# Scratch of the sample values laid out by batch: four loads a head in place of eight

## The chip, the cores and the metric

The kernel runs on one core of a Trainium2 chip. The metric is device time in microseconds for one whole execution. Engines are named as the profile names them: PE (TensorE, matrix products), DVE (VectorE), ACT (ScalarE), POOL (GpSimd) and SP (SyncE). In this kernel SP does no arithmetic: it issues the DMA transfers, one after the other, in the order in which they stand in its program.

## What is computed

One layer of a decoder step with two branches. A shared projection of the normed input gives, per head, queries, keys and values; the second branch keeps a matrix memory per head and advances it. Cut to what matters here:

```python
proj = jnp.einsum('btd,dn->btn', hn, w_in)
a_pool, z_pool, q, k, v, o, z_m, i_pre, f_pre, g_pool, g_mlstm = split_projection(proj)
...
kw = k * w_state[..., None]
C_new = decay[..., None, None] * C + jnp.einsum('bhsd,bhsv->bhdv', kw, v)
n_new = decay[..., None] * n + jnp.sum(kw, axis=2)
```

There are 528 prompt rows (512 and 16 meta tokens) of one sequence, and a sample group of 8 batches with 4 tokens each. Width 1024, four heads of 512. For the sample group each batch and head has its own state `C` of 512 x 512, read from memory, updated with four tokens and written back.

## The kernel before

Products are made with values split in two parts, a rounded one (`hi`) and the rest (`lo`), and three products hi x lo, lo x hi, hi x hi. So the update of one batch's `C` by its 4 tokens is one matmul over 12 rows: on one side `kwst` (weighted keys), on the other `vst` (values; parts hi, lo, hi, four tokens each):

```python
nc.tensor.matmul(pu, self.kwst[h, d][r:r + 12, g], self.vst[h][r:r + 12, g], start=True, stop=True,
                 tile_position=(r, 0))
```

Here `r` is 32 times the batch number modulo 4, and `g` is 0 for batches 0 to 3 and 1 for batches 4 to 7. So `vst` has four blocks of twelve partitions, and two batches in each.

The work goes head by head. `unit_v(h)` projects a head's values: it loads four pieces of weights (`wraw`), splits them, multiplies, and takes each result out of the accumulator into tiles `v` (`take`). When the last piece is done, five steps follow (`units[3].after`): two calls of `sample_rows`, two of `store` (values to the DRAM tensor `v_d`) and `stack`. The 32 sample rows (8 batches x 4 tokens) stand in two of the `v` tiles: 24 rows for batches 2 to 7 and 8 rows for batches 0 and 1. `sample_rows` splits them (L141 is the DVE half of the split) into tiles `vsp`, and writes hi, lo and hi again to a DRAM scratch `vs_d` of the head (L1013): six stores a head. `stack` reads the scratch into `vst` (L1019): eight loads a head, one for each batch.

Behind the values of a head come the projections of its queries, keys, gates. They are made in units that share one form (`quad`, L187 to 288): the weights come in two halves of 512 KB each, `ra` and `rb` (L196, two transfers). ACT and DVE split and combine them: ACT's casts at L203 and L210 (the first four blocks of `ra`, tile `w`), DVE's differences at L206 and L213 and sums at L216. PE multiplies (L167) in a fixed sequence of products; after some of them ACT copies the accumulator out (L239, tiles `p`, `u`, `e`), and DVE adds two of them up (L252 to 256, tiles `q`, `k`). Beside these units run the updates of the sample state: `C` is loaded (L1117) and stored (`out_dram`, L1149) in pieces of 512 KB, small rows of weights `sw` are loaded (L1040, L1041), and queries and their products go to DRAM (`q_d` L1049, `qc_d` L1167).

PE's order is written out by hand. For the other engines, and so for SP, a scheduler decides the order, from what waits for what and from the estimated lengths of instructions. Each engine then works strictly in its order. A DMA transfer is counted by one of eight semaphores that are taken in turn: a transfer that takes a semaphore waits until the transfer that had it before, eight transfers earlier, has landed.

Of the kernel before, what the change touches and what calls it, by code (L numbers as in the profile page):

```python
# [8 lines left out]
F32 = mybir.dt.float32  # L9
# [15 lines left out]
HD = 512  # L25
NB = 8
# [74 lines left out]
class Trunk:  # L101
# [857 lines left out]
    def unit_v(self, h):  # L959
        nc = self.nc  # L960
        V, A, G = nc.vector, nc.scalar, nc.gpsimd
        pv, vt, w = [], {}, {}

        def load(kk):
            w[kk] = [self.raw("wraw", 2, HD)]
            nc.sync.dma_start(w[kk][0], self.w_in[:, 2 * kk:2 * kk + 2, CV + h * HD:CV + (h + 1) * HD])

        def part(kk, low):
            if not low:
                w[kk] += [self.hl("w" + s, 2, HD) for s in ("hi", "lo")]  # L970
                A.copy(w[kk][1], w[kk][0])
            else:
                V.tensor_tensor(w[kk][2], w[kk][0], w[kk][1].bitcast(F32), ALU.subtract)

        def product(k, i):
            kk, k2 = divmod(k, 2)
            _, wh, wl = w[kk]
            if k == 0:
                pv.append(self.ps())
            if i < 4:  # L980
                c0 = COLS[i][0][2]
                hh, hl = (t[:, k, c0:c0 + P] for t in self.hT)
                for j, (s, m) in enumerate(((hl, wh), (hh, wl), (hh, wh))):
                    nc.tensor.matmul(pv[i], s, m[:, k2], start=(k == 0 and j == 0), stop=(k == 7 and j == 2))  # L984
            else:
                for j, m in enumerate((wl, wh)):
                    nc.tensor.matmul(pv[4][:112], self.hS[:, k], m[:, k2], start=(k == 0 and j == 0),  # L987
                                     stop=(k == 7 and j == 1))
            if k == 7:
                take(i)  # L990

        def take(i):
            t = vt[i] = self.r("v32")
            if i == 4:
                A.copy(t[:48, :HD], pv[4][64:112])
                V.tensor_tensor(t[:48, :HD], pv[4][:48], t[:48, :HD], ALU.add)
                A.activation(t[:48, :HD], t[:48, :HD], AF.Copy, accum_out=t[:48, HD:HD + 1])
            else:
                A.activation(t[:, :HD], pv[i], AF.Copy, accum_out=t[:, HD:HD + 1])

        def store(*rows):
            for i, r0, r1, n0 in rows:
                nc.sync.dma_start(self.v_d[h, n0:n0 + r1 - r0], vt[i][r0:r1, :HD + 1])


        def sample_rows(src, r0, r1, s0, n):
            d = vt.get("d")
            if d is None:
                d = vt["d"] = self.dram.tile([3, 32, HD], F32, name=f"vs_d{h}")
            hi, lo = (self.r("vsp", F32R)[:, :HD] for _ in range(2))  # L1010
            self.split(hi[r0:r1], lo[r0:r1], vt[src][r0:r1, :HD], A, V)
            for j, x in enumerate((hi, lo, hi)):
                nc.sync.dma_start(d[j, s0:s0 + n], x[r1 - n:r1].bitcast(F32))  # L1013

        def stack():
            vst = self.vst[h] = self.wp.tile([P, 2, HD], F32R, tag="vst", name=f"vst{h}", bufs=1)
            for b in range(NB):
                r = 32 * (b % 4)
                nc.sync.dma_start(vst[r:r + 12, b // 4].bitcast(F32), vt["d"][:, 4 * b:4 * b + 4])  # L1019

        units = []
        for kk in range(4):

            products = [lambda k=k, i=i: product(k, i) for k in (2 * kk, 2 * kk + 1) for i in range(5)] if kk < 3 else \
                [lambda k=k, i=i: product(k, i) for i in (4, 3, 0, 1, 2) for k in (6, 7)]
            units.append(Unit([lambda kk=kk: load(kk)], [lambda kk=kk: part(kk, False), lambda kk=kk: part(kk, True)],
                              products))
        units[3].after = [lambda: sample_rows(4, 0, 48, 8, 24), lambda: sample_rows(3, 96, 128, 0, 8),
                          lambda: store((4, 0, 24, 264), (4, 24, 48, 536), (3, 120, 128, 528), (3, 0, 120, 408)),
                          lambda: store((0, 0, 128, 8), (1, 0, 128, 136), (2, 0, 8, 0), (2, 8, 128, 288)), stack]  # L1030
        return units
# [624 lines left out]
```

## Time and profile before

| what | before |
|---|---|
| median of 3 runs | 1132.77 us (1131.75 to 1134.3) |
| profiled execution | 1128.94 us |
| its span, first to last instruction | 1127.2 us |
| mean granted clock of PE | 0.978 |
| PE busy | 1062.4 us, 94% of the span |
| DVE, ACT, POOL busy | 826.4, 542.7, 155.1 us |
| chain of work that ended last | PE 76%, DMA 12%, DVE 4%, ACT 3%, issue 2% |
| projections of the heads | about 60 to 745 us of the span |

The span is what the trace shows; the profiled execution's time includes what lies around it. "Busy" is time in which an engine has an instruction under way. A wait is named by what ended it: "PE ps L167 <- ACT u L239" is PE standing before the product at L167 until ACT's instruction on tile `u` at L239 was done. SP's lines are DMA issues; their length is SP's own time for the issue, and the transfer goes on behind it. The granted clock is the share of full speed that the throttle gave PE.

### The profile page before, as it was taken

How to read it: one execution, taken by the hardware profiler on the slowest of the kernel's cores; microseconds unless marked ns; L12 is line 12 of the kernel's file. 1: busy time of each engine (PE TensorE's matmuls, PEld its weight loads, DVE VectorE, ACT ScalarE, POOL GpSimd, SP SyncE). 2: the span in 40 equal slices, each digit the busy share in tenths (PEclk: the TensorE clock that was granted, in tenths of full speed). 3: DMA queues.
4: the chain of work that ended last, by engine and by line, in shares of the span. 5: the costliest groups of instructions: out<-in, count | busy, mean ns of one | idle time of the engine just before them, and what ended most of it. 6: DMA issues, size and time to landing. Idle time of an engine off the chain costs nothing.

```text
span 1127.2 us, 19656 instructions
## 1 busy us (share of the span) xinstructions
PE 1062.4 (94%) x7390; PEld 957.6 (85%) x7390; DVE 826.4 (73%) x1342; ACT 542.7 (48%) x1027; POOL 155.1 (14%) x309
## 2 busy tenths in 40 slices
PE   6799999999899999999999999987997889999997
PEld 5789999859899869999869989975986789999876
DVE  5778888786689687789696888864788988544343
ACT  5656555334454444454444554455676655122232
POOL 2100120001100001200000300012464423200000
PEclk9899999999999999999999999998999999999999
DMA  9263456789557688557587578888777889423232
GB/s 216 71 184 111 152 157 229 248 281 265 193 172 248 196 297 226 181 179 251 183 265 253 186 225 270 278 269 289 230 236 257 260 296 358 149 76 102 64 94 84
DMA packets 159663, 233.33 MB, mean 207 GB/s; under 512 B 17369, under 2 KB 82133, under 8 KB 159561
## 3 DMA queue, kind: packets, MB, share of 16 engines
q1 hardware_dynamic: 159569, 232.09, 64.1%
q8 instruction: 58, 0.95, 0.4%
q14 instruction: 36, 0.29, 0.1%
HBM read 160.65 MB, written 70.93 MB: 205 GB/s over the span
## 4 chain that ended last, share of the span: by engine, by line
PE 76%; DMA 12%; DVE 4%; ACT 3%; issue 2%; SPq 1%; POOL 1%; POOLq 0%; DVEq 0%; ACTq 0%
PE ps L167 57%; PE ps L984 7%; PE ps L1131 3%; PE ps L1372 2%; DMA wraw<-in_w_in_dram 2%; PE ps L1140 2%; DMA v_d<-v 1%; DMA rb<-in_w_in_dram 1%; DMA ra<-in_w_in_dram 1%; PE ps L987 1%; DMA v<-v_d 1%; DMA k<-k_d 1%; PE ps L1415 1%; PE ps L80 1%; ACT qc L1166 1%
## 5 line engine op out<-in xcount | busy, mean ns | idle before, releaser
L167 PE MATMUL ps<-hT_hi,w 128*128 128x272 f32 (+1 forms) x752 | 159.8, 294 | 0.0
L167 PEld LDWEIGHTS ps<-hT_hi,w 128*128 128x128 f32 x752 | 124.6, 190 | 4.9 <-issue 3.1
L167 PE MATMUL ps<-hT_lo,w 128*128 128x272 f32 (+1 forms) x376 | 109.2, 291 | 0.0
L1145 DVE SCALAR_TENSOR_TENSOR C<-C,sw,ps 128x512 f32<-128x512 f32 x128 | 89.5, 742 | 10.6 <-PE ps L1140 10.2
L167 PE MATMUL ps<-Sc_hi,wa 128*128 128x272 f32 (+1 forms) x376 | 81.0, 295 | 8.0 <-ACT u L239 7.9
L206 DVE TENSOR_TENSOR wb<-rb,wb 128x1024 fp32r<-128x1024 f32 x47 | 57.5, 1223 | 39.3 <-ACT wb L203 39.0
L167 PE MATMUL ps<-hT_hi,wb 128*128 128x272 f32 (+1 forms) x376 | 79.7, 291 | 3.5 <-DVE q L254 3.5
L167 PE MATMUL ps<-Sb_hi,wb 128*128 128x272 f32 (+1 forms) x376 | 80.1, 293 | 2.5 <-ACT p L239 1.9
L203 ACT CAST wa<-ra 128x1024 fp32r<-128x1024 f32 x47 | 49.3, 1049 | 63.8 <-DVE ra L216 56.6
L167 PE MATMUL ps<-Sd_hi,w 128*128 128x272 f32 (+1 forms) x376 | 79.6, 291 | 0.0
L167 PE MATMUL ps<-Sa_hi,wa 128*128 128x272 f32 (+1 forms) x376 | 78.7, 289 | 0.0
L167 PEld LDWEIGHTS ps<-hT_lo,w 128*128 128x128 f32 x376 | 71.3, 190 | 0.0
L167 PEld LDWEIGHTS ps<-Sc_hi,wa 128*128 128x128 f32 x376 | 63.4, 192 | 8.7 <-ACT u L239 8.6
L1054 POOL COPY qm<-qw 128x16 f32<-128x16 f32 x32 | 7.6, 271 | 426.4 <-DVE qw L1051 426.4
L167 PEld LDWEIGHTS ps<-hT_hi,wb 128*128 128x128 f32 x376 | 62.3, 189 | 4.2 <-DVE q L254 4.2
L203 ACT CAST w<-rb 128x1024 fp32r<-128x1024 f32 x47 | 49.3, 1050 | 33.3 <-PE ps L167 17.9
L167 PEld LDWEIGHTS ps<-Sb_hi,wb 128*128 128x128 f32 x376 | 62.3, 189 | 3.3 <-ACT p L239 2.3
L167 PEld LDWEIGHTS ps<-Sd_hi,w 128*128 128x128 f32 x376 | 62.8, 191 | 0.0
L167 PEld LDWEIGHTS ps<-Sa_hi,wa 128*128 128x128 f32 x376 | 62.0, 188 | 0.0
L206 DVE TENSOR_TENSOR w<-rb,w 128x1024 fp32r<-128x1024 f32 x47 | 57.4, 1222 | 3.7 <-ACT w L203 3.6
L206 DVE TENSOR_TENSOR wa<-ra,wa 128x1024 fp32r<-128x1024 f32 x47 | 57.3, 1218 | 0.0
L203 ACT CAST wb<-rb 128x1024 fp32r<-128x1024 f32 x47 | 49.1, 1046 | 15.6 <-DVE rb L216 15.4
(371 smaller groups left out, 3078.3 us busy)
## 6 DMA issues: line engine op xcount, KB each, us to landing
C<-in_state_C_dram SPq DMA_DIRECT2D x64, 512.0 KB
out_dram<-C SPq DMA_DIRECT2D x64, 512.0 KB
ra<-in_w_in_dram SPq DMA_DIRECT2D x47, 512.0 KB
rb<-in_w_in_dram SPq DMA_DIRECT2D x47, 512.0 KB
wraw<-in_w_in_dram SPq DMA_DIRECT2D x18, 512.0 KB
v<-v_d SPq DMA_DIRECT2D x32, 256.5 KB
wraw<-in_w_branch_mlstm_dram SPq DMA_DIRECT2D x16, 512.0 KB
k_d<-k SPq DMA_DIRECT2D x16, 280.0 KB
```

The source lines that it names most:

```text
L80: return self.tc.keep_in_program_order(getattr(self.engine, op)(*a, **k))
L167: self.nc.tensor.matmul(out, s, m, start=(first and j == 0), stop=(j == len(seq) - 1), skip_group_check=not check)
L203: A.copy(w[name][0], w[s])
L206: V.tensor_tensor(w[name][1], w[s], w[name][0].bitcast(F32), ALU.subtract)
L984: nc.tensor.matmul(pv[i], s, m[:, k2], start=(k == 0 and j == 0), stop=(k == 7 and j == 2))
L987: nc.tensor.matmul(pv[4][:112], self.hS[:, k], m[:, k2], start=(k == 0 and j == 0), stop=(k == 7 and j == 1))
L1131: nc.tensor.matmul(self.pqc[h][r:r + 8], self.qm[h % 2][:, d, b], Cs[bb // 2][:, bb % 2], start=(d == 0 and g == 0), stop=(d == 3 and g == 1),
L1140: nc.tensor.matmul(pu, self.kwst[h, d][r:r + 12, g], self.vst[h][r:r + 12, g], start=True, stop=True, tile_position=(r, 0))
L1145: V.scalar_tensor_tensor(C, C, self.bview(self.sw[h][:, 0])[:, 4 * g + bb, 3:4], pu, ALU.mult, ALU.add)
L1166: A.activation(t[r, :HD], pqc[r], AF.Copy, accum_out=t[r, HD:])
L1372: nc.tensor.matmul(pc, w[:, s, i], vr[i][:, m], start=(i == 0 and j == 0), stop=False)
L1415: nc.tensor.matmul(pb[:, o:o + mv.shape[-1] - m], s, mv[:, m:], start=(j == 0), stop=(j == last[True]))
```

## The change

The scratch of a head was [3, 32, 512]: part (hi, lo, hi), then the 32 rows, 4 to a batch. Now it is [8, 12, 512]: batch, then its twelve rows, part after part. A store of 24 rows wrote 24 consecutive rows; now it writes four rows into each of six batches. A load fetched one batch, four rows from each of three parts; now it fetches two batches, b and b + 4, each as twelve consecutive rows, into the two halves of one block of twelve partitions of `vst`. The contents of `vst` are the same. The number of stores stays at six a head, the loads go from eight to four.

```diff
@@ -1006,17 +1006,17 @@
         def sample_rows(src, r0, r1, s0, n):
             d = vt.get("d")
             if d is None:
-                d = vt["d"] = self.dram.tile([3, 32, HD], F32, name=f"vs_d{h}")
+                d = vt["d"] = self.dram.tile([NB, 12, HD], F32, name=f"vs_d{h}")
             hi, lo = (self.r("vsp", F32R)[:, :HD] for _ in range(2))
             self.split(hi[r0:r1], lo[r0:r1], vt[src][r0:r1, :HD], A, V)
             for j, x in enumerate((hi, lo, hi)):
-                nc.sync.dma_start(d[j, s0:s0 + n], x[r1 - n:r1].bitcast(F32))
+                nc.sync.dma_start(d[s0 // 4:(s0 + n) // 4, 4 * j:4 * j + 4], x[r1 - n:r1].bitcast(F32))
 
         def stack():
             vst = self.vst[h] = self.wp.tile([P, 2, HD], F32R, tag="vst", name=f"vst{h}", bufs=1)
-            for b in range(NB):
-                r = 32 * (b % 4)
-                nc.sync.dma_start(vst[r:r + 12, b // 4].bitcast(F32), vt["d"][:, 4 * b:4 * b + 4])
+            rows = vt["d"].rearrange("(g b) r e -> b r g e", g=2)
+            for b in range(4):
+                nc.sync.dma_start(vst[32 * b:32 * b + 12].bitcast(F32), rows[b])
```

The order of instructions on PE, DVE, ACT and POOL is the same before and after. SP's order changes around each head's scratch. First head 1, on SP, before: from the last scratch store (the eight `lo` rows) to the second pair `ra`, `rb` of the head's projections; the two `out_dram` transfers stand just ahead of it. A row is line, kind, destination<-source, shape of one piece, and a count.

```order
L1013 DMA vs_d_2876<-vsp_2906 8x512
L1117 DMA C_3617<-in_state_C_dram 128x2x512
L1019 DMA vst_2990<-vs_d_2876 12x1x512 x6
L1040 DMA sw_4796<-rows_d 128x32
L1049 DMA q_d<-q_450_2926 128x544
L1117 DMA C_3619<-in_state_C_dram 128x2x512
L1041 DMA sw_4796<-rows_d 128x32
L1019 DMA vst_2990<-vs_d_2876 12x1x512 x2
L1049 DMA q_d<-q_449_2925 128x544
L1117 DMA C_3901<-in_state_C_dram 128x2x512
L196 DMA ra_3160<-in_w_in_dram 128x4x256
L196 DMA rb_3162<-in_w_in_dram 128x4x256
```

The same place after:

```order
L1013 DMA vs_d_2872<-vsp_2902 2x4x512
L1019 DMA vst_2986<-vs_d_2872 12x2x512 x2
L1149 DMA out_dram<-C_2762 128x2x512
L1149 DMA out_dram<-C_2764 128x2x512
L1117 DMA C_3609<-in_state_C_dram 128x2x512
L1040 DMA sw_4788<-rows_d 128x32
L1041 DMA sw_4788<-rows_d 128x32
L1019 DMA vst_2986<-vs_d_2872 12x2x512 x2
L1049 DMA q_d<-q_450_2922 128x544
L1117 DMA C_3611<-in_state_C_dram 128x2x512
L1117 DMA C_3893<-in_state_C_dram 128x2x512
L1049 DMA q_d<-q_449_2921 128x544
L196 DMA ra_3152<-in_w_in_dram 128x4x256
```

Two of the loads have moved ahead of the two `out_dram` transfers, two stand behind both `sw`, and the eight-row store stands ahead of them all; the second `ra` still closes the stretch, with its `rb` behind it.

Head 2 on SP, before, from the second of two `out_dram` transfers to the second `ra` of the head:

```order
L1149 DMA out_dram<-C_4671 128x2x512
L1040 DMA sw_6739<-rows_d 128x32
L1013 DMA vs_d_4817<-vsp_4819 24x512
L1013 DMA vs_d_4817<-vsp_4846 8x512
L1041 DMA sw_6739<-rows_d 128x32
L1117 DMA C_5558<-in_state_C_dram 128x2x512
L1117 DMA C_5840<-in_state_C_dram 128x2x512
L1019 DMA vst_4929<-vs_d_4817 12x1x512 x8
L1049 DMA q_d<-q_770_4865 128x544
L1049 DMA q_d<-q_771_4866 128x544
L196 DMA ra_5099<-in_w_in_dram 128x4x256
```

And after:

```order
L1149 DMA out_dram<-C_4661 128x2x512
L1149 DMA out_dram<-C_4663 128x2x512
L1013 DMA vs_d_4809<-vsp_4811 6x4x512
L1013 DMA vs_d_4809<-vsp_4838 2x4x512
L1040 DMA sw_6727<-rows_d 128x32
L1041 DMA sw_6727<-rows_d 128x32
L1117 DMA C_5546<-in_state_C_dram 128x2x512
L1049 DMA q_d<-q_771_4858 128x544
L1117 DMA C_5828<-in_state_C_dram 128x2x512
L1019 DMA vst_4921<-vs_d_4809 12x2x512 x4
L1049 DMA q_d<-q_770_4857 128x544
L196 DMA ra_5087<-in_w_in_dram 128x4x256
```

The loads stay together, four in place of eight, and one `q_d` and the second `sw` have moved ahead of them; the two stores stand ahead of both `sw`.

## Rows read from the trace of the kernel before

**Rows 1.** The page, part 1: busy us (share of the span) xinstructions.
```profile
PE 1062.4 (94%) x7390; PEld 957.6 (85%) x7390; DVE 826.4 (73%) x1342; ACT 542.7 (48%) x1027; POOL 155.1 (14%) x309
```

**Rows 2.** Waits of PE in the projections: us in total, times, longest.
```profile
PE ps L167 <- ACT u L239: 7.9, 2, 4.1
PE ps L167 <- DVE q L254: 3.5, 3, 1.7
PE ps L167 <- ACT p L239: 1.9, 2, 1.4
```

**Rows 3.** Timeline of PE, head 1: start us, us, instruction [idle before <-releaser].
```profile
284.98 0.40 PE L167 MATMUL ps<-Sc_hi,wa 128*128 128x280 f32 x1 [4.14 <-ACT u L239]
```

**Rows 4.** Timeline of ACT, the same stretch.
```profile
284.00 0.62 ACT L210 CAST w<-ra 128x512 fp32r<-128x512 f32 x1 [5.70 <-DMA ra<-in_w_in_dram]
```

**Rows 5.** Timeline of SP, head 1.
```profile
259.06 1.50 SPq L1013 DMA_DIRECT2D vs_d<-vsp  x2
...
261.79 0.39 SPq L1013 DMA_DIRECT2D vs_d<-vsp  x1
...
266.73 5.92 SPq L1019 DMA_DIRECT2D vst<-vs_d  x6
...
273.39 0.34 SPq L1049 DMA_DIRECT2D q_d<-q  x1
...
274.81 1.44 SPq L1019 DMA_DIRECT2D vst<-vs_d  x2
...
277.27 0.45 SPq L196 DMA_DIRECT2D ra<-in_w_in_dram  x1
```

**Rows 6.** SP's issues of three lines: ns min/median/max, first and last start.
```profile
L1019 SPq DMA_DIRECT2D vst<-vs_d x32: 677/683/1177, 86.5 to 610.3; - x32
...
L1013 SPq DMA_DIRECT2D vs_d<-vsp x24: 263/294/1129, 79.0 to 606.0; - x24
...
L1167 SPq DMA_DIRECT2D qc_d<-qc x16: 263/298/657, 278.6 to 751.9; - x16
```

**Rows 7.** Timeline of SP, head 2.
```profile
437.61 1.61 SPq L1117 DMA_DIRECT2D C<-in_state_C_dram  x2
439.31 5.90 SPq L1019 DMA_DIRECT2D vst<-vs_d  x8
...
446.27 0.38 SPq L196 DMA_DIRECT2D ra<-in_w_in_dram  x1
```

**Rows 8.** Timeline of ACT, head 2.
```profile
452.53 0.62 ACT L210 CAST w<-ra 128x512 fp32r<-128x512 f32 x1 [5.32 <-DMA ra<-in_w_in_dram]
```

**Rows 9.** Windows around both stalls: busy by engine, then PEclk, DMA share, GB/s.
```profile
272.00:276.00 4.00, 4.00 (x34) 4.00 (x33) 3.87 (x6) 3.87 (x10) 1.07 (x4) 1.00 0.48 146
276.00:284.00 8.00, 4.84 (x38) 4.61 (x37) 2.92 (x5) 2.28 (x4) 1.48 (x8) 1.00 0.97 315
442.00:446.00 4.00, 4.00 (x34) 4.00 (x33) 3.39 (x6) 3.86 (x9) 0.59 (x2) 1.00 0.21 73
```

**Rows 10.** Windows after three stalls, for the granted clock.
```profile
78.50:82.00 3.50, 3.50 (x28) 3.50 (x28) 3.09 (x6) 3.43 (x6) 0.00 (x0) 1.00 0.63 111
285.83:289.24 3.41, 3.41 (x17) 3.41 (x16) 2.55 (x5) 1.05 (x1) 0.00 (x0) 0.50 0.88 279
289.24:292.65 3.41, 3.41 (x28) 3.41 (x28) 1.86 (x4) 2.24 (x3) 0.00 (x0) 1.00 0.28 105
603.27:606.68 3.41, 3.41 (x17) 3.41 (x16) 2.46 (x7) 2.25 (x4) 1.02 (x6) 0.50 1.00 315
```

**Rows 11.** Timeline of SP, head 3.
```profile
602.37 0.82 SPq L196 DMA_DIRECT2D ra<-in_w_in_dram  x1
...
608.66 0.43 SPq L196 DMA_DIRECT2D rb<-in_w_in_dram  x1
```

**Rows 12.** Timeline of ACT, head 3.
```profile
612.31 1.05 ACT L203 CAST w<-rb 128x1024 fp32r<-128x1024 f32 x1 [1.90 <-DMA rb<-in_w_in_dram]
```

**Rows 13.** Waits of SP in head 0: us in total, times, longest.
```profile
SPq L1019 <- DMA vs_d<-vsp: 3.8, 2, 2.3
```

## The prediction

> **What bounds the kernel now.** I read the page's busy times first: TensorE (PE) is busy 1062.4 of 1127.2 us [rows 1], so a change that touches no PE instruction can gain only where PE stands still, or where standing still costs it clock. The waits of PE in the projections (60 to 745 us) come next: two waits for ScalarE's (ACT) `u` copy make 7.9 us, three for VectorE's (DVE) `q` 3.5 us, two for ACT's `p` 1.9 us [rows 2]. That is 13.3 us in seven places. The largest is 4.14 us, just before 284.98, in the stage in which head 1 is projected [rows 3]; the other for `u` is then 7.9 - 4.1 = 3.8 us, in head 2.
>
> Why is `u` late? ACT works in order, and ahead of `u` stands the cast at L210, which waited 5.70 us for the weights `ra` to land, until 284.00 [rows 4]. The transfer of `ra` was issued only at 277.27, by SyncE (SP), the queue that issues all these transfers [rows 5]. It took 6.7 us to land; PE went on 0.98 us after that. SP itself was not waiting there: from 266.73 it issued six of the eight loads `vst<-vs_d` (5.92 us) and from 274.81 the other two (1.44 us), with other transfers between [rows 5]. One load costs 0.683 us of SP's time, a scratch store 0.294 [rows 6]; six loads at 0.683 are 4.1, the rest of the 5.92 is mostly waiting for older transfers, since each transfer takes one of eight semaphores in turn and so waits until the eighth before it has landed. Head 2 is the same picture: eight loads from 439.31 (5.90 us) with nothing between them, two `q_d`, then `ra` at 446.27 [rows 7], which lands 6.2 us later, when ACT's cast at 452.53 ends an idle time of 5.32 us [rows 8]. Meanwhile the DMA engines were half empty: busy 0.48 and 0.21 of the time in the 4 us before `ra`, 0.97 after it [rows 9].
>
> The clock adds to it. From 285.83, right after the 4.14 us stall, PE was granted 0.50 (1.2 GHz of 2.4) for 3.41 us and did 17 matmuls, and 28 in the next 3.41 at full clock; after the 1.75 us stall at 602.09 it was 0.50 too, but after the stall of 1.4 us near 77 it stayed at 1.00 [rows 10]. By the counts one such stretch costs 3.41 x 11/28 = 1.3 us, by the level 3.41/2 = 1.7; I take 1.5. Head 2's stall has such a stretch as well (the row of 285.83 stands for both).
>
> **The change part by part.** Compute order is untouched on PE, DVE, ACT and GpSimd; only SP's sequence and the shape of 24 stores and 32 loads change.
>
> *Loads, 32 to 16.* Today a load reads three groups of four rows and writes twelve partitions: its two sides are cut differently, and it costs 0.683 us. After, both sides are 12 x 2 x 512. The nearest forms with sides cut alike are the present stores, 0.294, and `qc_d<-qc`, 0.298 [rows 6]. I take 0.33. The bounds are 0.29 and, if a load of twice the rows costs twice as much, 1.37.
>
> *Stores, still 24.* Their two sides are cut alike today (24 x 512) and differently after (24 rows against 6 x 4). The nearest row for sides cut differently is today's load: I take 0.68, bounds 0.29 and 0.68. Per head SP pays 6 x 0.39 = 2.3 us more for stores and 8 x 0.683 - 4 x 0.33 = 4.1 less for loads: 1.8 less in all. But place matters more than the sum. The stores stand before the first `ra`, where SP is not short of time: two of them from 259.06 fill 1.50 us with 0.6 us of issuing [rows 5], the rest is waiting for older transfers. So I cost them at nothing; if that cover were gone, it would be 2.3 us a head on the first `ra`.
>
> *Head 1.* Two loads now stand before the two `out_dram` transfers and two behind `sw`. In the new order the last thing to hold `ra` is a chain of older transfers: `q_d`, just ahead, waits for the load of `C` that today lands at about 273.3, since today's `q_d` waited for that and went out at 273.39 [rows 5]. One `q_d` (0.34) later `ra` goes: at 273.85, 3.4 us earlier. Ahead of it are then two loads of `C` (1.05 MB) and two `q_d` (0.56 MB), with itself 2.1 MB; at the 315 GB/s of the full stretch [rows 9] that is 6.7 us from 273.4, so 280.1; by today's 6.7 us after issue 280.6. PE would go on at 281.1 to 281.6 in place of 284.98, and it is ready at 280.84: of 4.14 us about 0.5 stay. **Saved 3.6.**
>
> *Head 2.* The second `C` load still goes at 438.8 (today two fill 437.61 to 439.22 [rows 7]). Four loads at 0.33 to 0.68, each with 0.05 between, and one `q_d` follow, so `ra` goes at 441.2 to 442.5; today 446.27. With 6.2 us it lands at 447.4 to 448.7. Today PE goes on 0.98 after ACT's cast of 452.53 [rows 8], at 453.5, after 3.8 us of standing, so it ran out of work at 449.7 and would need `ra` 0.98 before that, at 448.7. **Saved 3.8.** This place doesn't hang on the price of a load, as long as it isn't above 0.7.
>
> *Head 3.* `ra` 602.37, then six loads and a store, `rb` at 608.66 [rows 11]; ACT waited 1.90 us for that `rb` [rows 12], and the smaller wait for `p` (1.9 - 1.4 = 0.5 [rows 2]) follows from it. Now only two loads stand between `ra` and `rb`. **Saved 0.5.** The 1.75 us stall there waits for DVE behind a `v_d` landing; it stays, and its half clock.
>
> *Head 0.* SP waited 3.8 us for stores to land before it could load [rows 13], but PE has no wait for `ra` or `rb` there. Saved 0.
>
> *Clock.* Without the stalls of 4.14 and 3.77 both half-clock stretches go: **3.0**. What is next after a stall that is gone: PE is fed by itself then, the casts behind wait for PE.
>
> Sum: 3.6 + 3.8 + 0.5 + 3.0 = 10.9 us. Profiled execution 1128.94 - 10.9 = 1118.0; its span 1127.2 would be about 1116.3. The median of the runs, 1132.77, lies 3.83 above the profiled one; I keep that offset: **1121.9 us**.
>
> **The rivals.**
>
> *B, half a cure.* `ra` lands at 282 rather than 280.5 (other transfers ahead of it), and a stall of some 1.8 us stays in head 1, about that which at 602.09 still brought the half clock [rows 10]. Then 1.3 less is saved there and 1.5 of the clock stays: 1124.7.
>
> *E, the change doesn't do what it says.* If issuing goes by rows moved, a load costs 1.37 us and four as much as eight. The four in head 2 then take 5.7, `ra` goes at 445.3 and 0.9 is saved; in head 1, where two stand earlier, some 2.2; clock 0 to 1.5. About 1129. Against it: 128 x 4 x 256 weights (`ra`) are issued in 0.45 and 0.38 us [rows 5, 7], so rows alone don't make the price.
>
> *C, the stores' landing takes the loads' place: no change.* Head 1's first load now stands in front of the `out_dram` and `C` transfers, and must wait until the scratch stores have landed; behind it SP and so `ra` wait. Up to a landing at about 264.5 nothing is lost, from there each microsecond moves `C` and `ra` by up to one, and at 268.5, 7.5 us after the store's issue near 261, the gain in head 1 is eaten. In head 2 the load stands at 439.3, 5 us after the last store, and 4.5 us more eat the gain there. A landing about 9 us after issue gives +1.5 in head 1, -1.0 in head 2: 1133; with less, down to 1130.5. For it: in head 0 the loads waited 3.8 us for just this [rows 13], and a store now cut into 6 x 4 may take longer. Against it: head 1's store of 261.79 had landed by 266.73, within 4.9 us, since the load there went without idle time [rows 5].
>
> By the Trainium skill, page "DMA: Bandwidth & Descriptors", section "Why a DMA increments its semaphore by 16 and not by 1", a transfer runs on the largest number of engines up to 16 that divides the slowest dimension of both its sides. By that rule the stores go from 12 and 8 engines to 6 and 2, the loads from 3 to 12; this speaks against the change. An estimate from that page's rule: either store then puts 8 KB on an engine where `ra` puts 32 KB, so the landing moves by some tenths of a microsecond and the sum by as little. No view here shows single DMA engines.
>
> *D, slower.* The same mechanism past its point: were the landing 12 us after issue, head 1 loses 4.5 and head 2 2.0 us: 1139. It decides from about 9.5 us on; no scratch store in these rows comes near.
>
> **How the numbers follow.** Forecast A 0.62, with a range of its own of 1118.5 to 1125: the upper end keeps one half-clock stretch and a microsecond of stall. B 0.10, E 0.08, C 0.12, D 0.07, and 0.01 for things I don't see. Upwards in gain: the stalls that hang on SP's loads wholly gone (4.1 + 3.8 + 0.5) and the clock at 1.7 each give 11.8, so 1121.0; were head 3's stall of 1.75 and its half clock to go as well, 1117.7. Hence the lower end, 1117.5. The upper end, 1130, takes in B and E: together 0.80. A measurement here tells 0.2%, 2.3 us, from no change. Faster 0.80, same 0.12, slower 0.08.
>
> **What would show it.** In the profile after: `vst<-vs_d` x16 at 0.3 to 0.4 us and `vs_d<-vsp` x24 near 0.68; the second `ra` of head 1 issued near 274 and of head 2 near 442; ACT's L210 there idle under 2 us; PE's waits for `u` under 1 us in all; no granted clock of 0.50 near 286 and 453, but still near 603. I am wrong if `ra` goes as late as today although the loads are cheap (then look for SP's waits for `vs_d` stores), if it goes early and lands late (the DMA engines were the bound), or if PE then stands at the next unit instead.

## The result, and the profile after

The changed kernel took 1125.1 us (median of 12 runs, 1122.12 to 1131.95) against 1132.94 us (12 runs): a ratio of 0.9926, 95% interval 0.9906 to 0.9946, or 6 to 11 us less. The forecast was 1121.9 us, a gain of 10.9; the measured gain is 7.8. The profiled execution's span is 1122.3 us against 1127.2.

SP's issues of the loads (L1019) and stores (L1013) in the changed kernel, ns min/median/max, first and last start, answering to [rows 6]:

```profile
L1019 SPq DMA_DIRECT2D vst<-vs_d x16: 302/364/1197, 87.8 to 605.5; - x16
```
```profile
L1013 SPq DMA_DIRECT2D vs_d<-vsp x24: 603/677/825, 80.1 to 598.9; - x24
```

The prices came out as the prediction took them: a load 0.364 us (taken: 0.33; before: 0.683), a store 0.677 (taken: 0.68; before: 0.294). The 0.677 stands between two kinds of store: the twelve of 24 rows have a median of 0.736 us, the twelve of 8 rows of 0.619. Per head that is 6 x 0.677 + 4 x 0.364 = 5.5 us of issuing in place of 7.2.

PE's waits in the projections, as [rows 2] (us in total, times, longest):

```profile
PE ps L167 <- ACT u L239: 3.2, 2, 2.4
PE ps L167 <- DVE q L254: 3.2, 2, 2.9
PE ps L167 <- ACT p L239: 1.4, 1, 1.4
```

The 7.9 us before `u` are 3.2; the other two groups together are 0.8 less. Where the 3.2 are: PE's timeline in head 1, and ACT's there and in head 2, as [rows 3], [rows 4] and [rows 8]:

```profile
282.10 0.40 PE L167 MATMUL ps<-Sc_hi,wa 128*128 128x280 f32 x1 [2.43 <-ACT u L239]
```
```profile
281.13 0.62 ACT L210 CAST w<-ra 128x512 fp32r<-128x512 f32 x1 [3.99 <-DMA ra<-in_w_in_dram]
```
```profile
444.94 0.62 ACT L210 CAST w<-ra 128x512 fp32r<-128x512 f32 x1 [1.63 <-DMA ra<-in_w_in_dram]
```

Head 1 keeps 2.43 of its 4.14 us. Head 2's stall is gone: ACT waited 1.63 us for `ra` in place of 5.32, and PE not at all. SP's timelines in head 1 and head 2, as [rows 5] and [rows 7]:

```profile
264.75 0.76 SPq L1019 DMA_DIRECT2D vst<-vs_d  x2
...
266.52 1.07 SPq L1117 DMA_DIRECT2D C<-in_state_C_dram  x1
...
269.73 0.81 SPq L1019 DMA_DIRECT2D vst<-vs_d  x2
...
271.72 1.17 SPq L1117 DMA_DIRECT2D C<-in_state_C_dram  x2
274.84 0.34 SPq L1049 DMA_DIRECT2D q_d<-q  x1
275.28 0.38 SPq L196 DMA_DIRECT2D ra<-in_w_in_dram  x1
```
```profile
433.84 0.38 SPq L1117 DMA_DIRECT2D C<-in_state_C_dram  x1
...
435.31 1.85 SPq L1019 DMA_DIRECT2D vst<-vs_d  x4
437.27 0.34 SPq L1049 DMA_DIRECT2D q_d<-q  x1
438.13 0.40 SPq L196 DMA_DIRECT2D ra<-in_w_in_dram  x1
```

The four loads in head 2 take 1.85 us where eight took 5.90, and `ra` follows 2.82 us after they begin, in place of 6.96. In head 1 the second `ra` goes at 275.28 and not at 273.85, as forecast: `q_d`, just ahead of it, stood until 274.84 for a load of `C` issued at 266.52, which so took 8.3 us to land. Before, the one issued at 266.23 had landed by 273.39, 7.2 us later. But 0.75 of these 1.43 us only tell that everything in this trace stands later: the PE product that starts at 245.01 in the trace of before starts at 245.76 here.

The granted clock (last columns: PEclk, DMA share, GB/s) after head 1's stall of 2.43 us, in the next stretch, and behind head 2's place:

```profile
283.20:286.60 3.40, 3.40 (x17) 3.40 (x16) 2.43 (x4) 1.05 (x1) 0.00 (x0) 0.50 0.92 290
286.60:290.00 3.40, 3.40 (x28) 3.40 (x28) 1.79 (x4) 2.40 (x3) 0.00 (x0) 0.99 0.24 93
447.00:451.00 4.00, 4.00 (x33) 4.00 (x32) 3.87 (x8) 2.24 (x3) 1.48 (x3) 1.00 0.82 263
```

It fell to 0.50 there again, for 3.4 us, as in [rows 10]; after head 2, where PE didn't stand, it stayed at 1.00.

One trace of each kernel doesn't tell how much of this is the change. There are three of the changed kernel (the two more are after2 and after3, below) and two of the kernel before (before2). The three columns `late2` are kernels with the loads at another place, described below. The table gives the time between the starts of the same PE instructions in each trace (those that stand at 245, 275, ... us in the first trace of before; PE's order is the same in all), in us:

| from, to | before | before2 | after | after2 | after3 | late2_before | late2_after | late2_t |
|---|---|---|---|---|---|---|---|---|
| 245 to 275 | 30.05 | 31.97 | 28.12 | 27.55 | 28.95 | 29.82 | 29.54 | 29.85 |
| 275 to 300 (head 1, second `ra`) | 24.95 | 25.19 | 23.23 | 21.32 | 20.42 | 19.19 | 19.73 | 20.25 |
| 300 to 420 | 120.29 | 120.33 | 120.26 | 120.25 | 120.29 | 120.29 | 120.28 | 120.27 |
| 420 to 460 (head 2) | 39.79 | 35.83 | 33.81 | 35.17 | 37.01 | 34.53 | 33.81 | 35.71 |
| 460 to 590 | 129.94 | 129.98 | 129.94 | 129.94 | 129.94 | 129.94 | 129.94 | 129.94 |
| 590 to 620 (head 3) | 29.99 | 30.26 | 31.22 | 30.59 | 31.28 | 30.19 | 31.16 | 29.02 |
| sum 245 to 620 | 375.0 | 373.6 | 366.6 | 364.8 | 367.9 | 364.0 | 364.5 | 365.0 |
| 790 to 920 (attention) | 130.01 | 133.60 | 131.93 | 133.60 | 132.25 | 133.29 | 133.29 | 130.70 |

The two stretches of this stage without a scratch in them (300 to 420 and 460 to 590) agree to 0.1 us. The sum of the stage that the change touches is 374.3 us in the mean before and 366.4 after: 7.9 us, which is the gain of the medians (7.8). That the two meet so closely is in part chance: the five traced spans differ by only 5.4 us in the mean (1128.1 and 1122.7), and from 745 to 790, which is not in the table, the changed kernel took 46.2, 47.0 and 47.1 us where the kernel before took 45.1 and 45.0. Whether that is the change isn't shown; late2_after, with the same stores and loads, took 45.1. The attention stage, which gave back 1.9 us in the first pair of traces, takes 130.0 and 133.6 us in two executions of the same kernel before; so that is no effect of the change. The windows rows of that stage show that the granted clock differs (PEclk is the third column from the end, 0.97 and 0.95), first before, then before2; the third fence is the changed kernel:

```profile
245.00:620.00 375.00, 361.88 (x2570) 322.87 (x2569) 290.82 (x459) 174.89 (x316) 22.22 (x77) 0.99 0.70 225
790.00:920.00 130.00, 115.36 (x751) 103.74 (x750) 107.94 (x185) 85.93 (x190) 60.71 (x84) 0.97 0.76 250
```
```profile
245.00:620.00 375.00, 362.70 (x2583) 323.69 (x2582) 292.86 (x463) 175.31 (x317) 23.59 (x83) 0.99 0.72 226
790.00:920.00 130.00, 113.88 (x720) 102.33 (x720) 104.91 (x180) 84.18 (x186) 60.47 (x81) 0.95 0.76 249
```
```profile
245.00:620.00 375.00, 368.33 (x2634) 329.48 (x2633) 298.94 (x473) 179.42 (x323) 26.38 (x85) 0.99 0.72 230
```

In a window of the same 375 us PE stood still 6.7 us in the changed kernel (375 - 368.33), where it had stood 13.1 and 12.3.

### The profile page after: what moved, and what is told of

It is laid out like the page before. It is cut to its first block, busy times and chain, and to the rows that moved or that the text cites. A ratio compares the mean times of both kernels' runs of the same rounds, so it can differ in the third digit from the quotient of the medians.

```text
span 1122.3 us, 19632 instructions
## 1 busy us (share of the span) xinstructions
PE 1064.3 (95%) x7390; PEld 959.8 (86%) x7390; DVE 826.9 (74%) x1342; ACT 542.1 (48%) x1027; POOL 152.5 (14%) x309
## 4 chain that ended last, share of the span: by engine, by line
PE 74%; DMA 12%; DVE 5%; ACT 4%; issue 2%; SPq 2%; POOL 1%; POOLq 0%; DVEq 0%; ACTq 0%
PE ps L167 57%; PE ps L984 7%; PE ps L1131 3%; DMA v_d<-v 2%; PE ps L1372 2%; PE ps L1140 1%; DMA v<-v_d 1%; DMA ra<-in_w_in_dram 1%; PE ps L987 1%; DMA kw<-k_d 1%; PE ps L80 1%; DMA wraw<-in_w_in_dram 1%; DMA x<-in_x_prompt_dram 1%; DMA k<-k_d 1%; PE ps L1415 1%
## 5 line engine op out<-in xcount | busy, mean ns | idle before, releaser
L203 ACT CAST wa<-ra 128x1024 fp32r<-128x1024 f32 x47 | 49.3, 1050 | 62.3 <-DVE ra L216 52.8
```

What stands on the lines that cost most here:

```text
L203: A.copy(w[name][0], w[s])
```

## The experiments

One theory and three rivals. The theory of the prediction: what costs are SP's loads ahead of the second `ra` of a head, by place and price. Rival one: the number of transfers costs, since each takes a turn on one of eight semaphores. Rival two: the scheduler's new order on SP brought the gain, not the price of loads. Rival three: the dear stores cost as well, so that the change gives back a part. Ratios are to the kernel before in the same rounds.

**The same kernels again** (before2, after2, after3; no edit).

> The kernel before once more, for a second trace beside the first. If the attention stage's 130.0 us of the first trace (790 to 920 us) is what this kernel always takes, it comes back within 0.5; if it varies between executions, it comes out at 131 to 134 us as in the other five traces. The stalls before `u` in heads 1 and 2 come back at 3 to 5 us.

> The changed kernel once more, on the chip and in the rounds of the next three, and with a second trace. If the 2.4 us that still stand before `u` in head 1, the 2.9 us before `q` in head 3 and the 3 us that the attention stage (745 to 920 us) gave back belong to the change, they come back within some tenths. If they are run-to-run variation, the attention stage differs by 2 us or more between the two traces of the same kernel. Time: 0.990 to 0.995 of the kernel before.

> The changed kernel a third time, beside the next three in the same rounds and with a third trace: 0.990 to 0.996 of before; between 245 and 620 us 114 to 117 us in place of 123 to 125, the rest of the span as the traces of before within their own spread.

Measured: after2 0.9932 (0.9908 to 0.9955), after3 0.9932 (0.9914 to 0.995), beside the first 0.9926. The attention stage (790 to 920) of the changed kernel differed by 1.7 us between the first two traces, a little under the 2 us expected of run-to-run variation; before2, with 3.6 us against before, shows the variation. The four stretches around the scratches in after3 sum to 117.7 us, a little above the 114 to 117 expected. In before2 the stall before `u` in head 1 was 3.61 us, in head 2 only 2.06, below what was expected, and the clock stayed up after the latter, which took 36 in place of 40 us for that stretch. Here are the stall and the clock behind it, first in the trace of before, then in before2:

```profile
453.50 0.60 PE L167 MATMUL ps<-Sc_hi,wa 128*128 128x280 f32 x1 [3.77 <-ACT u L239]
453.08:456.50 3.42, 3.00 (x13) 3.00 (x14) 2.08 (x3) 0.93 (x4) 0.00 (x0) 0.50 0.82 250
```
```profile
451.69 0.40 PE L167 MATMUL ps<-Sc_hi,wa 128*128 128x280 f32 x1 [2.06 <-ACT u L239]
```
```profile
452.00:460.00 8.00, 8.00 (x64) 8.00 (x63) 6.44 (x11) 4.44 (x7) 0.00 (x0) 1.00 0.66 212
```

In the changed kernel head 1's stall was 2.43, 2.04 and 1.14 us and was followed by a half clock only in the first; in head 3 the stall before `q` was 2.88, 2.26 and 1.48, another before `u` 0.81, 0.58 and 2.02. So stalls of one to four microseconds differ between executions by one to two, and whether one is followed by a half clock differs with them.

**t_major: cheap stores and cheap loads.** With the twelve rows in the order token, part (the keys' side changed alike, in one line of copies on POOL), both sides of every transfer are cut alike. The edit is shown against the changed kernel.

```diff
-                d = vt["d"] = self.dram.tile([NB, 12, HD], F32, name=f"vs_d{h}")
+                d = vt["d"] = self.dram.tile([32, 3, HD], F32, name=f"vs_d{h}")
...
-                nc.sync.dma_start(d[s0 // 4:(s0 + n) // 4, 4 * j:4 * j + 4], x[r1 - n:r1].bitcast(F32))
+                nc.sync.dma_start(d[s0:s0 + n, j], x[r1 - n:r1].bitcast(F32))
...
-            rows = vt["d"].rearrange("(g b) r e -> b r g e", g=2)
+            rows = vt["d"].rearrange("(g b t) j e -> b (t j) g e", g=2, b=4)
...
-                G.tensor_copy(stq[:, :, 4 * i:4 * i + 4], self.bview(src))
+                G.tensor_copy(stq[:, :, i:i + 10:3], self.bview(src))
```

> Scratch laid out token by token, [32, 3, 512], with the twelve rows of a block in the order token, part on both sides of the product: stores and loads then have both sides cut alike. Every theory expects stores at 0.29 us and four loads a head at 0.36. Theory (the loads ahead of the second `ra` cost, the stores are hidden): within 1.5 us of the changed kernel. Rival (the dear stores cost too, on `v_d` and the first `ra` of a head): 1.5 to 4 us faster than the changed kernel, the stall before `q` in head 3 back at 1.75 us.

Measured: 0.9948 (0.9928 to 0.9968), 1125.67 us beside after2's 1123.19 in the same rounds. Stores 0.290 us, loads 0.367. Stores at less than half the price brought nothing, so rival three's 1.5 to 4 us didn't come; but 2.5 us more than the changed kernel's median is outside the theory's 1.5 us too (the two intervals overlap). The kernels differ in more than the stores: the scheduler put SP's order otherwise, so this run alone doesn't settle rival three. SP's timeline in head 1:

```profile
271.80 0.90 SPq L1117 DMA_DIRECT2D C<-in_state_C_dram  x2
273.67 0.74 SPq L1019 DMA_DIRECT2D vst<-vs_d  x2
274.50 0.35 SPq L1049 DMA_DIRECT2D q_d<-q  x1
274.95 0.40 SPq L196 DMA_DIRECT2D ra<-in_w_in_dram  x1
```

The second pair of loads now stands directly ahead of the second `ra` and has to wait for a `C` load to land; `ra` goes at 274.95, and PE stood 3.41 us, against 1.14 to 2.43 in the changed kernel. Here cheap transfers in a worse place were worth no more than dear ones in a better.

**batch8: the cheap form, but eight loads.** The new scratch, one load for each batch; the edit is shown against the changed kernel.

```diff
-            rows = vt["d"].rearrange("(g b) r e -> b r g e", g=2)
-            for b in range(4):
-                nc.sync.dma_start(vst[32 * b:32 * b + 12].bitcast(F32), rows[b])
+            for b in range(NB):
+                r = 32 * (b % 4)
+                nc.sync.dma_start(vst[r:r + 12, b // 4].bitcast(F32), vt["d"][b])
```

> The new scratch with one load for each batch: eight loads a head of the cheap form, dear stores as in the changed kernel. Theory (the form of a load makes its price): 0.30 us a load, 2.4 us a head against 5.5 before and 1.5 in the changed kernel; the second `ra` of head 2 near 442 or a microsecond behind the changed kernel, and 1 to 2.5 us slower than the changed kernel, still 0.993 to 0.997 of before. Rival (the number of transfers, each with its turn on a semaphore, makes the price): no more than 0.2% from the kernel before.

Measured: 0.9988 (0.9971 to 1.0006); a load costs 0.362 us. The theory's time was missed and rival one's came out: the cheap form alone brought 0.1%, within the interval of nothing. Whether it came out for rival one's reason is another question. SP's timeline in head 1 and in head 2:

```profile
265.55 2.60 SPq L1019 DMA_DIRECT2D vst<-vs_d  x6
269.39 0.40 SPq L1149 DMA_DIRECT2D out_dram<-C  x1
269.83 1.20 SPq L1019 DMA_DIRECT2D vst<-vs_d  x2
271.08 0.40 SPq L1149 DMA_DIRECT2D out_dram<-C  x1
...
275.92 0.42 SPq L196 DMA_DIRECT2D ra<-in_w_in_dram  x1
```
```profile
438.46 5.61 SPq L1019 DMA_DIRECT2D vst<-vs_d  x8
...
445.43 0.40 SPq L196 DMA_DIRECT2D ra<-in_w_in_dram  x1
```

In head 2, where SP's order is the changed kernel's but for the number, `ra` follows 6.97 us after the first load, as in the kernel before (6.96), not 2.82. Eight loads of 0.36 are 2.9 us, but they take 5.61: the last three stood until the transfer that had had their semaphore, eight transfers earlier, had landed. SP's waits from 436 to 447 us, and PE's before `u`:

```profile
SPq L1019 <- DMA C<-in_state_C_dram: 1.9, 2, 1.4
SPq L1019 <- DMA q_d<-q: 0.4, 1, 0.4
```
```profile
450.33 0.40 PE L167 MATMUL ps<-Sc_hi,wa 128*128 128x280 f32 x1 [0.74 <-ACT u L239]
```

So a load costs SP its price and its turn, and four have half the turns. But in head 2 that cost PE little: it stood 0.74 us, since `ra` landed 3.9 us after its issue (6.3 in the kernel before), and the stretch 420 to 460 took 34.7 us, no more than the changed kernel's 35.3 in the mean. What batch8 lost against the changed kernel shows in head 1 (275 to 300: 26.2 us against 21.7), where PE stood 5.52 us before `u`, and there the order is another too: six loads stand ahead of `out_dram`, and the two transfers of 512 KB go at 269.39 and 271.08, where the kernel before had sent them between the first `rb` and 265.15. Number and order aren't told apart there, so that the number of loads costs the kernel time is not shown.

**dear_both: dear stores and eight dear loads, in nearly the new order.** Four rows of each batch padded to five in the old scratch; the edit is shown against the kernel before.

```diff
-                d = vt["d"] = self.dram.tile([3, 32, HD], F32, name=f"vs_d{h}")
+                d = vt["d"] = self.dram.tile([3, NB, 5, HD], F32, name=f"vs_d{h}")
...
-                nc.sync.dma_start(d[j, s0:s0 + n], x[r1 - n:r1].bitcast(F32))
+                nc.sync.dma_start(d[j, s0 // 4:(s0 + n) // 4, 0:4], x[r1 - n:r1].bitcast(F32))
...
-                nc.sync.dma_start(vst[r:r + 12, b // 4].bitcast(F32), vt["d"][:, 4 * b:4 * b + 4])
+                nc.sync.dma_start(vst[r:r + 12, b // 4].bitcast(F32), vt["d"][:, b, 0:4])
```

> The old scratch with each batch's four rows padded to five, so that stores are cut differently as in the changed kernel, and the eight loads as before: 14 dear issues a head, 9.5 us of SP in place of 7.2. SP's order comes out much like that of the changed kernel (stores ahead of `sw`, one `q_d` ahead of the loads). Theory (the price of the loads): the stalls before `u` in heads 1 and 2 stay at 3 us or more, 0.998 to 1.004 of before. Rival (the new order brought the gain, not the price): 0.992 to 0.996 of before, head 2 without its stall.

Measured: 1.0032 (1.0014 to 1.005). PE's waits in the projections, and the one in head 2:

```profile
PE ps L167 <- ACT u L239: 8.7, 2, 5.9
```
```profile
452.42 0.40 PE L167 MATMUL ps<-Sc_hi,wa 128*128 128x280 f32 x1 [2.75 <-ACT u L239]
```

With old prices and the changed kernel's order around the stores the kernel is 0.3% slower than before, 0.9% slower than the changed one. In head 2, where SP's order is the changed kernel's but for the number of loads, the stall was 2.75 us, a little under the 3 us expected and between the two of the kernel before; in batch8 it was 0.74, in the changed kernel 0.08, 0.22 and none. There rival two falls, as far as one trace tells. In head 1 it is not tested: all eight loads stand ahead of the two `out_dram`, which is not the changed kernel's order, and the stall was 5.9 us.

**late_before, late_after, late_t: the loads behind the second `ra` and `rb`.** In the kernel before, the changed one and t_major, `stack` is called one stage later, behind the second `q` unit, and its loads keep that place on SP. The edit is shown for the kernel before.

```diff
-                nc.sync.dma_start(vst[r:r + 12, b // 4].bitcast(F32), vt["d"][:, 4 * b:4 * b + 4])
+                self.tc.keep_in_program_order(
+                    nc.sync.dma_start(vst[r:r + 12, b // 4].bitcast(F32), vt["d"][:, 4 * b:4 * b + 4]))
...
-                          lambda: store((0, 0, 128, 8), (1, 0, 128, 136), (2, 0, 8, 0), (2, 8, 128, 288)), stack]
+                          lambda: store((0, 0, 128, 8), (1, 0, 128, 136), (2, 0, 8, 0), (2, 8, 128, 288))]
+        self.stack = stack
...
-        u = self.quad_out(self.wcols(CQ + h * HD + 256 * j), tiles, after=[lambda: rows(0), lambda: rows(1)])
+        u = self.quad_out(self.wcols(CQ + h * HD + 256 * j), tiles, after=[lambda: rows(0), lambda: rows(1)] + ([self.stack] if j == 1 else []))
```

> The kernel before with its eight dear loads moved behind the second `ra` and `rb` of the head (and behind `qc_d`), stores, layout and number of loads as before. Theory (the loads cost because they stand ahead of the second `ra` on SP): the stalls before `u` in heads 1 and 2 fall under 1.5 us each, 5 to 10 us faster than before, 0.991 to 0.996, as much as the changed kernel. Rival (SP has too much to issue, wherever it stands, or the number of transfers is what costs): a stall of 2 us or more comes back at the third `ra`, and no more than 0.2% from before.

> The changed kernel (dear stores) with its four loads moved behind the second `ra` and `rb`. Theory: as the kernel above within 1 us, since the stores are hidden. Rival (the dear stores delay the first `ra` and `v_d`): 1.5 to 3 us slower than the kernel above.

> Scratch token by token (cheap stores, four cheap loads) and the loads moved behind the second `ra` and `rb`. Theory: no stall over 1 us before `u` in heads 1 and 2, and no half clock there; 1 to 4 us faster than the changed kernel, 0.988 to 0.993 of before. Rival (what still holds the second `ra` of head 1 is the landing of `C` and `out_dram` through the eight semaphores, not the loads): the stall in head 1 stays at 2 us or more, and the time is within 1.5 us of the changed kernel.

Measured: 0.9949 (0.9928 to 0.997), 0.9939 (0.9919 to 0.9959), 0.9949 (0.993 to 0.9968). late_before's time is as the theory had it, though a stall of over 1.5 us came in head 1; late_t missed its 0.988 to 0.993. The "kernel above" of late_after's expectation is late_t: late_after was 1.2 us faster than it, not within 1 us and not 1.5 to 3 slower. In all three the stretch 275 to 300 took 19.0 us, in place of 25.0: the stall and the half clock of the second `ra` in head 1 were wholly gone, with the old loads too. But a new stall stood before `u` of an earlier unit: 2.94, 1.77 and 3.66 us in head 1, 4.84, 5.57 and 4.94 in head 3. ACT's timeline in late_before, head 1:

```profile
252.70 0.61 ACT L210 CAST w<-ra 128x512 fp32r<-128x512 f32 x1
258.75 0.61 ACT L138 CAST vsp<-v 32x512 fp32r<-32x512 f32 x1 [5.44 <-DMA v_d<-v]
259.39 0.40 ACT L239 ACTIVATE u<-ps 128x272 f32<-128x272 f32 x1
```

The scheduler had moved a cast of `vsp` (L138), which waits for a `v_d` transfer, ahead of `u`: with one step less in the list, the others were written out earlier. The next three keep the step, and ACT's order with it.

**late2_before, late2_after, late2_t: the same, ACT's order kept.** An empty step takes the place of `stack` in its list, and the call goes into the last step of the second `q` unit. The loads keep their place in program order as in the last three; the rest of the edit:

```diff
-                          lambda: store((0, 0, 128, 8), (1, 0, 128, 136), (2, 0, 8, 0), (2, 8, 128, 288)), stack]
+                          lambda: store((0, 0, 128, 8), (1, 0, 128, 136), (2, 0, 8, 0), (2, 8, 128, 288)), lambda: None]
+        self.stack = stack
...
+        stack = self.stack
+
+        def last():
+            rows(1)
+            if j == 1:
+                stack()
-        u = self.quad_out(self.wcols(CQ + h * HD + 256 * j), tiles, after=[lambda: rows(0), lambda: rows(1)])
+        u = self.quad_out(self.wcols(CQ + h * HD + 256 * j), tiles, after=[lambda: rows(0), last])
```

> The kernel before with its eight dear loads behind the second `ra` and `rb`, as in the run late_before, but with the order of ACT left as it is in the kernel before (in late_before a cast of `vsp` that waits for a `v_d` transfer had come ahead of `u`). Theory (the place of the loads on SP is what costs): 275 to 300 us takes 19 us as in late_before, the new stalls before `u` at 257 and 588 go, no stall before `u` over 1 us in heads 1 and 2; 0.988 to 0.994 of before, at least as fast as the changed kernel. Rival (another order of SP only moves the wait, to the first `ra` of a head): one stall over 2.5 us before `u` or `q` comes back in each head, 0.994 to 0.998.

> The changed kernel with its four loads behind the second `ra` and `rb`, ACT's order as before. Theory: the 2 us that were left of the stall in head 1 go, with the half clock: 1 to 4 us faster than the changed kernel. Rival: within 1 us of it, the time lost in head 3 (590 to 620) or at the first `ra`.

> Cheap stores and four cheap loads (scratch token by token), loads behind the second `ra` and `rb`, ACT's order as before. Theory (place counts, and the price no longer does once the loads are out of the way): within 1.5 us of late2_before and late2_after. Rival (price counts everywhere on SP): at least 1.5 us faster than late2_before.

Measured, in the rounds in which the changed kernel had 0.9932 (1125.11 us): late2_before 0.9893 (0.987 to 0.9917), 1120.85 us; late2_after 0.9888 (0.9865 to 0.991), 1120.39 us; late2_t 0.9905 (0.9888 to 0.9922), 1121.48 us. PE's waits in late2_before, then SP's loads and its timeline in head 1:

```profile
PE ps L167 <- DVE q L254: 4.5, 3, 2.7
...
PE ps L167 <- ACT p L239: 1.4, 1, 1.4
```
```profile
L1020 SPq DMA_DIRECT2D vst<-vs_d x32: 679/684/814, 129.6 to 610.0; - x32
```
```profile
268.79 0.99 SPq L1125 DMA_DIRECT2D C<-in_state_C_dram  x2
269.83 0.46 SPq L1051 DMA_DIRECT2D q_d<-q  x1
270.39 0.38 SPq L196 DMA_DIRECT2D ra<-in_w_in_dram  x1
...
275.80 3.55 SPq L1020 DMA_DIRECT2D vst<-vs_d  x3
...
279.86 3.60 SPq L1020 DMA_DIRECT2D vst<-vs_d  x5
283.56 0.40 SPq L196 DMA_DIRECT2D ra<-in_w_in_dram  x1
```

No wait for `u` is left (the line left out, 3.5 us, stands at 742.9, behind the projections, and is in every trace there; in head 1, late2_after has one of 0.45 us and late2_t one of 0.98). The eight loads cost 0.684 us each, as they always did, and stand behind `ra` (270.39), where ACT and PE have their weights for the next unit; the third `ra` at 283.56 comes in time. The order on PE, DVE, ACT and POOL is that of the kernel before, so the place on SP is the cause. In these kernels price and number matter only as long as the loads stand where `ra` waits behind them: three kernels with loads at 0.68 x 8 and 0.36 x 4, stores at 0.29 and 0.68, lie within 1.1 us of each other. This beats both kernels: some 12 us less than before and 4 less than the changed one by the medians. By the table's sums it is 1.4 to 2.4 us less than the changed one in this stage, so the sign is surer than the size. Almost none of it is in head 1: from 245 to 300 these three took 49.0, 49.3 and 50.1 us, the changed kernel 49.9 in the mean, so there the changed kernel gained about as much.

late2_after is 4.7 us faster than the changed kernel by the medians, a little more than the 1 to 4 expected. The rival of late2_before spoke of a stall over 2.5 us in each head. In head 3 there is one before `q` (2.74 and 2.79 us in late2_before and late2_after); that one hangs on `v_d`, and the kernel before has it too, a microsecond shorter (1.75 and 1.93).

## Why the prediction was right, and where it was off

**What bounds the stage** held: two stalls before `u`, made by SP's loads ahead of the second `ra`. late2_before shows it, with the other engines' order unchanged: without the loads there, with their old price, both stalls are gone. "SP itself was not waiting there" goes too far: three of the six loads in head 1 stood about 0.5 us each until `rb` and two `out_dram` had landed.

**The prices** held, load and store (0.364 and 0.677), and nothing shows that **the stores cost** time: late2_t with cheap stores was no faster than late2_after, and t_major, in another order, no faster than the changed kernel.

**Head 2** held: `ra` landed so that PE didn't wait (a stall of 3.77 gone, 0.08 left), and in the first pair of traces the stretch gave 6.0 us (39.8 to 33.8). But its worth was mis-sized, since 3.77 us and a half clock were one execution's: before2 had 2.06 and none. And in after2 and after3 PE stood 0.99 and 1.75 us before `q` there. The stretch 420 to 460 is 37.8 us in the mean of two before and 35.3 in the mean of three after: 2.5 us, not 3.8 + 1.5.

**Head 1** held at `ra` and failed in a term taken over from the first trace: that PE is ready at 280.84. The traces start at different times, so the table counts from the PE product that stands at 245.01 in the first trace of before, in us:

| head 1 | forecast | before | before2 | after | after2 | after3 |
|---|---|---|---|---|---|---|
| second `ra` issued | 28.84 | 32.26 | 33.53 | 29.52 | 28.29 | 29.49 |
| PE has no more work | 35.83 | 35.83 | 37.75 | 33.90 | 33.33 | 34.73 |
| PE goes on | 36.1 to 36.6 | 39.97 | 41.36 | 36.34 | 35.38 | 35.87 |

PE went on when it was forecast to, or up to 0.7 us sooner. But it had run out of work 1.1 to 2.5 us sooner than taken, and so stood 2.43, 2.04 and 1.14 us where 0.5 was forecast. It was ready sooner because 245 to 275 is 2.8 us shorter (31.0 to 28.2 in the mean), which I had at nothing. The two belong together: a part of what is gained there is lost in waiting for `ra`. From 245 to 300 the gain is 6.2 us in the mean (56.1 to 49.9), where 3.6 + 1.5 were forecast; the half clock came in one of three traces.

Rival B's time (1124.7) is the nearest to the measured one, and the stall that it left (1.8 us) is near these, but that is luck: it let `ra` land late, at 282. In the first trace ACT began on `ra` at 281.13, which is 280.4 on the scale of before, as forecast (280.1 to 280.6).

**Why 245 to 275 is shorter** stays open. In the changed kernel's first trace the stall of 1.03 us for a `C` load near 250 is gone and the next one, before `q`, is 0.30 in place of 1.09. Neither the stores nor the number of loads makes it alone: batch8 has the same stores and took 30.1, t_major has four loads and took 29.9, late2_after has both and took 29.5.

**Head 3** was expected 0.5 us faster and is 0.9 slower (30.1 to 31.0 in the mean). There are two stalls there, before `q` and before `u`. Whether dear stores ahead of `v_d` and `ra` make it isn't settled: with cheap stores late2_t took 29.0 and late2_after, with dear ones, 31.2, but t_major, which has cheap ones as well, took 31.9.

So 6.2 + 2.5 - 0.9 = 7.8 by the traces' means, where 5.1 + 5.3 + 0.5 = 10.9 were forecast: the sum was 2.8 too high in head 2 and 1.4 in head 3, and 1.1 too low in head 1. That the time lies in the range owes something to the 2.8 us that weren't forecast. Two of the signs failed in the first trace: ACT's L210 in head 1 stood 3.99 us (under 2 was said), and PE's waits for `u` make 3.2 us (under 1), the larger with a clock of 0.50 behind it.

**The rivals.** E (a price by rows) falls by the prices. C and D (the stores' landing) fall where they would have decided: in heads 1 and 2 SP has no wait for a `vs_d` store. The loads at 264.75 don't wait for the store just ahead of them (264.02) but for those of 257.05 and 259.36, by the semaphores; the pair at 269.73 waits for it, and it had landed by then, within 5.7 us, where C needed 7.5 to eat the gain. In head 2 the last store had landed within 5.6 us. In head 3 SP has one such wait; of its waits in the changed kernel from 585 to 614 us:

```profile
SPq L1019 <- DMA vs_d<-vsp: 2.9, 1, 2.9
```

It stands ahead of the second pair of loads, which went 6.2 us after the store that they waited for, and PE didn't wait for the `ra` behind it. So the mechanism is there, but cost nothing here. The rule on how many engines a transfer takes, cited there from the Trainium skill, page "DMA: Bandwidth & Descriptors", section "Why a DMA increments its semaphore by 16 and not by 1", is neither borne out nor contradicted, since no view shows single engines. That the number of loads matters beside their price was in the prediction only as a wait within the 5.92 us, not as a cause of its own. batch8 shows that it costs SP time (5.61 us for eight loads of 0.36); that it costs the kernel time isn't shown.

## What to carry to other kernels

When a small transfer stands in a queue ahead of one that a busy engine waits for, look first whether it can stand behind it: here that was worth more (12 us by the medians) than making it cheaper and halving its number (8 us). If it must stay, count what it costs the issuing engine, which here went with whether both of its sides are cut alike, and its turn on the completion semaphores, which each transfer takes: in batch8 three of eight loads stood 2.3 us in all for it. A stall that is left need not mean that the weights come late: PE may have come sooner. And take stalls from two or three traces before adding them up: these differed by up to two microseconds between executions, and brought a half clock in some and not in others.

## What the runs showed of the hardware

- SP's time for one issue went with the way the two sides are cut, and much less with rows: medians of 0.26 to 0.37 us where they are cut alike (8 x 512, 24 x 512, 12 x 512, 12 x 2 x 512), of 0.62 to 0.74 where not (0.619 for 8 rows against 2 x 4, 0.683 for 12 against 3 x 4, 0.736 for 24 against 6 x 4).
- A stall of 2.06 us was not followed by a half clock in one execution, one of 1.75 was in another, in the changed kernel 2.43 was and 2.04 was not, and in dear_both 2.75 was not. The length of the stall alone doesn't tell.
